# Prompt attention: the probabilities of two key blocks are transposed in a row, and weighted in a row

## The chip, the cores and the metric

The kernel runs on one core of one Trainium2 chip. The metric is the device time of one execution in microseconds (us); lower is better. The engines of a core run side by side, each through its own list of instructions in order, and wait for each other by semaphores: TensorE (PE, matrix products and its weight loads PEld), VectorE (DVE), ScalarE (ACT), GpSimd (POOL) and SyncE (SP), which here only starts DMA transfers.

## The reference

Two layers of an encoder trunk (width 1024). Each layer projects the normalised input once, feeds four branches with it (a recurrent branch, latent attention, spatial gating, pooling), gates them and projects back. There are 1024 prompt tokens and 8 groups of 16 sample tokens, 1152 in all. The change touches the attention of the prompt:

```
def mla_attend(q_nope, q_rope, qpos, k_nope, krope, v, kpos):
    s = (einsum('bqhd,bkhd->bhqk', q_nope, k_nope)
         + einsum('bqhd,bkd->bhqk', q_rope, krope)) / sqrt(96)
    mask = (qpos // 64)[:, None] >= (kpos // 64)[None, :]
    s = where(mask, s, -1e30)
    pr = softmax(s, axis=-1)
    return einsum('bhqk,bkhd->bqhd', pr, v)
```

Four heads, queries in 8 blocks of 128, values 64 wide per head, all in fp32. Block `qt` of queries sees keys up to `(qt + 1) * 128`.

## The kernel before

Tokens lie in columns, in three groups of 384. A layer goes through its input projections (one 128-wide piece of features after the other, `project`, L245), with the branches' own work strung between them, then through the prompt attention, then through the output projection. The prompt attention is the loop at L1394 to L1412.

Its unit is a row: one query block of one head (32 rows, L1260). A row has one or two key blocks of up to 512 keys. `scores(r)` (L1269) multiplies queries by keys on TensorE into PSUM tiles `b` (four of them), finds the maximum on VectorE (`mx`, `ng`), and takes the exponential on ScalarE (L1295) into one of four slots of probabilities (`Pb`, printed as X). A new row is started only when as many slots are free as it has key blocks.

`turn(u, b)` (L1299) takes key block `b` of two rows (two heads, `hh` 0 and 1) and transposes the probabilities on TensorE, 128 by 128 at a time, into PSUM tiles `pj`, of which there are two: one for each head. The head 0 tile is copied to SBUF by VectorE (L1311), the head 1 tile by ScalarE (L1313), into a ring of four tiles `PTb` (L1195).

`weigh(u, b)` (L1316) multiplies the transposed probabilities by the values, into the PSUM tile `st` that holds the outputs of a pair of query blocks. For each 128 keys there are two products (L1325), one per head. Each has 64 output rows: head 0 goes to partitions 0 to 63, head 1 to 64 to 127. `settle` (L1330) divides by the sums and gates the result when a pair of query blocks is done.

The order in the program: for each (u, b), first the scores of as many rows as fit, then `weigh` of the turn before, then `turn`. A scheduler in the framework then places the instructions of each engine; it can set an instruction ahead of others when it finds its inputs ready earlier, so what stands in an engine's list is not the program's order word for word. There are 24 turns per layer, an even number for each pair of query blocks.

Of the kernel before, what the change touches and what calls it, by code (L numbers as in the profile page):

```python
# [48 lines left out]
def tile_trunk(ctx: ExitStack, tc: tile.TileContext, *aps):  # L49
# [25 lines left out]
    def mm(out, lhsT, rhs, start=True, stop=True):  # L75
        return PE.matmul(out, lhsT=lhsT, rhs=rhs, start=start, stop=stop, skip_group_check=True)  # L76
# [39 lines left out]
    def st():  # L116
        return ps_st.tile([128, 512], F32, tag="st", name=nm("st"))
# [7 lines left out]
    def go(lane, gen):  # L125
        lanes.setdefault(lane, deque()).append(gen)
# [15 lines left out]
    def tick():  # L142
        for lane in list(lanes):
            step(lane)

    def finish(*names):
        while any([step(n) for n in names]):
            pass
# [196 lines left out]
    for l in range(L):  # L345
# [919 lines left out]
        def widths(qt):  # L1265
            n = (qt + 1) * 128
            return [min(512, n - 512 * b) for b in range((n + 511) // 512)]

        def scores(r):  # L1269
            pr, s, h = rows[r]  # L1270
            qt = pr[s]
            if h == 0 and s == 0:
                sums[pr] = smp.tile([128, 2, 2, 4], F32, tag="sums", name=nm("sums"), bufs=2)
                Po.memset(sums[pr], 0.0)
            mx = smp.tile([128, 2], F32, tag="mx", name=nm("mx"), bufs=4)
            banks = []
            ws = widths(qt)
            for b, w in enumerate(ws):
                pc = pb()
                mm(pc[:, :w], qcols(h, qt * 128, 128), Kt[h][:, 512 * b:512 * b + w])  # L1280
                if b == len(ws) - 1:
                    V.memset(pc[0:64, w - 64:w], NEG)
                V.tensor_reduce(out=mx[:, b:b + 1], in_=pc[:, :w], axis=AX.X, op=ALU.max)  # L1283
                banks.append((pc, w))
            ng = smp.tile([128, 1], F32, tag="ng", name=nm("ng"), bufs=4)
            if len(ws) == 2:
                V.tensor_scalar(out=ng, in0=mx[:, 0:1], scalar1=mx[:, 1:2], scalar2=-SCALE,  # L1287
                                op0=ALU.max, op1=ALU.mult)
            else:
                V.tensor_scalar(out=ng, in0=mx[:, 0:1], scalar1=-SCALE, scalar2=None, op0=ALU.mult)  # L1290
            prow[r] = []
            for b, (pc, w) in enumerate(banks):
                slot = free.pop(0)
                P = Pb[slot]
                A.activation(out=P[:, :w], in_=pc[:, :w], func=AF.Exp, scale=SCALE, bias=ng,  # L1295
                             accum_out=sums[pr][:, b, s, h:h + 1])
                prow[r].append((slot, w))

        def turn(u, b):  # L1299

            trow[u, b] = []
            for hh in range(2):
                slot, w = prow[2 * u + hh][b]
                ptp = pj()
                for j in range(w // 128):
                    PE.transpose(ptp[:, j * 128:(j + 1) * 128], Pb[slot][:, j * 128:(j + 1) * 128], ident)  # L1306
                free.append(slot)
                PT = PTb[ring["t"] % len(PTb)]
                ring["t"] += 1
                if (hh if w > 128 else u % 2) == 0:  # L1310
                    V.tensor_copy(out=PT[:, :w], in_=ptp[:, :w])  # L1311
                else:
                    A.activation(out=PT[:, :w], in_=ptp[:, :w], func=AF.Copy)  # L1313
                trow[u, b].append(PT)

        def weigh(u, b):  # L1316
            pr, s, h = rows[2 * u]
            if h == 0 and s == 0 and b == 0:
                St["po"] = st()
            o = St["po"][:, s * 256 + h * 64:s * 256 + h * 64 + 128]  # L1320
            pts = trow.pop((u, b))
            n = pr[s] + 1
            for j in range(4 * b, min(4 * b + 4, n)):
                for hh in range(2):
                    mm(o[64 * hh:64 * hh + 64], Vt[j][:, (h + hh) * 64:(h + hh + 1) * 64],  # L1325
                       pts[hh][:, j % 4 * 128:j % 4 * 128 + 128], j == 0, j == n - 1)
            if h == 2 and s == 1 and 4 * b + 4 >= n:
                go("f", settle(pr, St["po"]))

        def settle(pr, po):  # L1330

            sm = sums.pop(pr)
            V.tensor_tensor(out=sm[:, 0], in0=sm[:, 0], in1=sm[:, 1], op=ALU.add)
            V.reciprocal(out=sm[:, 0], in_=sm[:, 0])
            Po.tensor_copy(out=Ob[0].rearrange("p (a f) -> p a f", a=8),
                           in_=sm[:, 0].rearrange("p s h -> p (s h)").unsqueeze(2).broadcast_to([128, 8, 64]))
            yield
            pt = pj()
            for j in range(4):
                PE.transpose(pt[:, j * 128:(j + 1) * 128], Ob[0][:, j * 128:(j + 1) * 128], ident)  # L1340
            A.activation(out=Ob[1], in_=pt, func=AF.Copy)
            V.tensor_tensor(out=Ob[1], in0=po, in1=Ob[1], op=ALU.mult)
            for j in range(4):
                s, i = divmod(j, 2)
                gs = gB[i][:, pr[s] * 128:pr[s] * 128 + 128]
                Po.tensor_tensor(out=gs, in0=gs, in1=Ob[1][:, j * 128:(j + 1) * 128], op=ALU.mult)
# [23 lines left out]
        def operand(g):  # L1370
            if g == 2:
                finish("f")
            h = xp.tile([128, 8, G], F32R, tag="xh", name=nm("yh"))
            lo = xp.tile([128, 8, G], F32R, tag="xl", name=nm("yl"))
            for n, k in enumerate(out_order):
                if k < 2:
                    src = AR[k][g][:, :, 0, :]
                    hv, lv_ = chv(h[:, k, :]), chv(lo[:, k, :])
                else:
                    if k < 4:  # L1380
                        src = gB[k - 2][:, gcols(g)]
                    else:
                        src = s_tile("ea", EA)
                        SY.dma_start(out=src, in_=ysp[:, k - 4, gcols(g)])
                    hv, lv_ = h[:, k, :], lo[:, k, :]
                A.activation(out=hv, in_=src, func=AF.Copy)
                eng = Po if k % 2 else V
                eng.tensor_tensor(out=lv_, in0=src, in1=hv.bitcast(F32), op=ALU.subtract)
                if n == 3:
                    yield  # L1390
            yh.append(h)
            yl.append(lo)

        ahead, before = 0, None  # L1394
        for u in range(16):
            for b in range(len(widths(rows[2 * u][0][rows[2 * u][1]]))):
                while ahead < 32 and len(widths(rows[ahead][0][rows[ahead][1]])) <= len(free):
                    scores(ahead)
                    ahead += 1
                if before:  # L1400
                    weigh(*before)
                turn(u, b)
                before = u, b
                tick()
            if u == 8:
                finish("q")
            if u == 12:
                go("o", operand(0))
                go("o", operand(1))
        weigh(*before)  # L1410
        finish("n")
        go("o", operand(2))  # L1412

# [191 lines left out]
```

## Time and profile before

| | |
|---|---|
| median of 3 runs | 1441.29 us (1440.91 to 1446.11) |
| profiled execution | 1443.43 us |
| its span in the trace | 1441.6 us |
| TensorE busy | 1357.0 us (94%) |
| VectorE, ScalarE, GpSimd busy | 779.5, 747.8, 466.8 us |
| prompt attention, layer 1 | about 551 to 635 us of the span |
| prompt attention, layer 2 | about 1255 to 1338 us of the span |

The trace is of the profiled execution. Its time has 1.83 us around the span (launch and end). A product in fp32 stands in the trace as two matrix instructions, so a run of 8 products of `weigh` is a row with x16; a transposition is one instruction. Short idle times of TensorE show in the distance between starts, since the ends of matrix instructions are modelled.

### The profile page before, as it was taken

The page shows a single profiled execution, that of the slowest core. Times are in us where ns is not written, and L with a number is a line of the kernel's source. Part 1 is how long each engine was busy: PE and PEld are TensorE (multiplying, and loading weights), DVE is VectorE, ACT ScalarE, POOL GpSimd, SP SyncE. Part 2 cuts the span into 40 slices and gives each one's busy share as a digit, 9 for nine tenths or more (in the row PEclk, how much of TensorE's full clock was granted, in tenths as well). Part 3 has the DMA queues.
Part 4 walks back from the last instruction along what each step waited for, and adds up shares of the span by engine and source line. Part 5 has one row for each costly group of instructions (what it writes and reads, how often), then busy time and mean ns, then how long its engine had stood idle before and what let it go on. Part 6 is the DMA issues. An engine that isn't in the chain of part 4 may idle for free.

```text
span 1441.6 us, 26906 instructions
## 1 busy us (share of the span) xinstructions
PE 1357.0 (94%) x9962; PEld 1157.6 (80%) x9962; DVE 779.5 (54%) x1758; ACT 747.8 (52%) x2013; POOL 466.8 (32%) x600
## 2 busy tenths in 40 slices
PE   4799989999999998999989998999999999899999
PEld 3678878888988886679977788788789788766998
DVE  6875954435235567752287858444532375777211
ACT  6762234655466677652257621555653676766210
POOL 4514404426411023232162333332653111422320
PEclk9899999999999999999999999999999999999999
DMA  7212241210211213033300123321122111131222
GB/s 222 53 34 70 67 101 42 65 46 25 92 50 65 66 37 118 15 103 106 93 29 30 47 67 68 89 70 50 32 73 68 53 58 58 47 101 45 76 93 77
DMA packets 116596, 97.40 MB, mean 68 GB/s; under 512 B 46129, under 2 KB 111345, under 8 KB 116465
## 3 DMA queue, kind: packets, MB, share of 16 engines
q1 hardware_dynamic: 76776, 73.74, 17.8%
q10 hardware_dynamic: 39688, 21.94, 5.1%
q8 instruction: 79, 1.29, 0.4%
q14 instruction: 53, 0.43, 0.1%
HBM read 71.48 MB, written 24.16 MB: 66 GB/s over the span
## 4 chain that ended last, share of the span: by engine, by line
PE 67%; DVE 17%; DMA 5%; ACT 4%; issue 3%; POOL 3%; SPq 0%; ACTq 0%; DVEq 0%; POOLq 0%
PE pj L76 40%; PE b L76 14%; PE st L76 8%; DMA nd<-ns 3%; PE pj L1306 3%; DVE ea L278 2%; DVE m L540 2%; DVE m L542 2%; DMA tt<-dd 1%; POOL sp L99 1%; PE b L588 1%; DVE gn L730 1%; DVE ea L170 1%; DMA m<-nds 1%; DVE m L793 1%
## 5 line engine op out<-in xcount | busy, mean ns | idle before, releaser
L76 PE MATMUL pj<-xh,wh 128*128 128x384 f32 x1152 | 415.1, 361 | 19.3 <-ACT xh L280 7.3
L76 PE MATMUL pj<-xl,wh 128*128 128x384 f32 x1152 | 395.6, 343 | 3.8 <-POOL xl L282 2.8
L76 PE MATMUL pj<-xh,wl 128*128 128x384 f32 x1152 | 395.7, 344 | 0.0
L242 POOL TENSOR_TENSOR wl<-wr,wh 128x256 fp32r<-128x256 f32 x200 | 159.4, 805 | 459.6 <-ACT wh L241 398.0
L76 PEld LDWEIGHTS pj<-xh,wh 128*128 128x128 f32 x1152 | 220.9, 192 | 44.4 <-ACT sho L400 13.5
L76 PEld LDWEIGHTS pj<-xl,wh 128*128 128x128 f32 x1152 | 221.1, 192 | 12.1 <-POOL xl L282 4.8
L76 PEld LDWEIGHTS pj<-xh,wl 128*128 128x128 f32 x1152 | 220.6, 192 | 4.3 <-issue 3.1
L76 PE MATMUL pj<-yh,wh 128*128 128x384 f32 x384 | 129.3, 337 | 2.4 <-DVE x L1428 2.4
L76 PE MATMUL pj<-yh,wl 128*128 128x384 f32 x384 | 128.6, 335 | 0.0
L76 PE MATMUL pj<-yl,wh 128*128 128x384 f32 x384 | 128.3, 334 | 0.0
L241 ACT ACTIVATE wh<-wr 128x256 fp32r<-128x256 f32 x200 | 81.3, 414 | 80.7 <-PE pj L76 38.7
L242 POOL TENSOR_TENSOR wl<-m,wh 128x256 fp32r<-128x256 f32 x56 | 43.5, 789 | 102.8 <-ACT wh L241 84.9
L76 PEld LDWEIGHTS pj<-yh,wh 128*128 128x128 f32 x384 | 72.1, 188 | 3.7 <-DVE x L1428 2.7
L76 PEld LDWEIGHTS pj<-yl,wh 128*128 128x128 f32 x384 | 72.1, 188 | 0.1
L76 PEld LDWEIGHTS pj<-yh,wl 128*128 128x128 f32 x384 | 72.1, 188 | 0.1
L1295 ACT ACTIVATE X<-b,ng 128x512 f32<-128x512 f32 (+3 forms) x96 | 55.0, 577 | 25.6 <-DVE ng L1287 21.4
L76 PE MATMUL b<-sp,cr 128*128 128x384 f32 (+3 forms) x192 | 59.5, 385 | 3.2 <-POOL sp L99 2.8
L1283 DVE TENSOR_REDUCE mx<-b 128x1 f32<-128x512 f32 (+3 forms) x96 | 53.0, 555 | 9.7 <-PE b L76 8.0
L76 PEld LDWEIGHTS st<-X,X 128*64 128x64 f32 x576 | 35.1, 136 | 27.4 <-ACT X L1313 7.6
L1424 DVE TENSOR_TENSOR pt<-pj,pt 128x384 f32<-128x384 f32 x24 | 13.4, 557 | 80.6 <-PE pj L76 80.6
L241 ACT ACTIVATE wh<-m 128x256 fp32r<-128x256 f32 x56 | 22.2, 412 | 60.9 <-PE pj L76 59.2
L1306 PE MATMUL pj<-cm,X 128*128 128x128 f32 x288 | 48.0, 286 | 5.2 <-ACT X L1295 5.2
(307 smaller groups left out, 2584.9 us busy)
## 6 DMA issues: line engine op xcount, KB each, us to landing
wr<-in_win_dram SPq DMA_DIRECT2D x176, 128.0 KB
m<-in_wout_dram SPq DMA_DIRECT2D x12, 512.0 KB
x<-in_xT_dram SPq DMA_DIRECT2D x12, 384.0 KB
ysp<-m ACTq DMA_DIRECT2D x24, 192.0 KB
pt<-in_xT_dram SPq DMA_DIRECT2D x24, 192.0 KB
ea<-ysp SPq DMA_DIRECT2D x24, 192.0 KB
x1d<-x ACTq DMA_DIRECT2D x24, 192.0 KB
pt<-x1d SPq DMA_DIRECT2D x24, 192.0 KB
```

What stands on the lines that cost most here:

```text
L76: return PE.matmul(out, lhsT=lhsT, rhs=rhs, start=start, stop=stop, skip_group_check=True)
L99: by[1].tensor_tensor(out=view(lo), in0=src, in1=view(hi.bitcast(F32)), op=ALU.subtract)
L170: V.tensor_tensor(out=acc, in0=acc, in1=q, op=ALU.add)
L241: A.activation(out=h, in_=r, func=AF.Copy)
L242: Po.tensor_tensor(out=lo, in0=r, in1=h.bitcast(F32), op=ALU.subtract)
L278: V.scalar_tensor_tensor(out=t, in0=xs[k // 2][:, k % 2, :], scalar=vcs[:, l, V_NG + k:V_NG + k + 1], in1=rs, op0=ALU.mult, op1=ALU.mult)
L540: V.tensor_tensor(out=tm, in0=full[:, 0:s + 1, s:s + 1].broadcast_to([np_, s + 1, w]), in1=NTt[0:np_, s:s + 1, s + 1:n].broadcast_to([np_, ...
L542: V.tensor_tensor(out=full[:, 0:s + 1, s + 1:n], in0=full[:, 0:s + 1, s + 1:n], in1=tm, op=ALU.add)
L588: PE.transpose(pt[:, i * 128:(i + 1) * 128], KB[i][g][:, cl].rearrange("p a t -> p (a t)"), ident)
L1283: V.tensor_reduce(out=mx[:, b:b + 1], in_=pc[:, :w], axis=AX.X, op=ALU.max)
L1295: A.activation(out=P[:, :w], in_=pc[:, :w], func=AF.Exp, scale=SCALE, bias=ng, accum_out=sums[pr][:, b, s, h:h + 1])
L1306: PE.transpose(ptp[:, j * 128:(j + 1) * 128], Pb[slot][:, j * 128:(j + 1) * 128], ident)
```

## The change

`weigh` is no longer called for one turn ahead of each next turn, but for the two turns before, ahead of every second turn. So the lists of `weigh` come in pairs, and so do the turns.

```
-        ahead, before = 0, None
+        ahead, before, turns = 0, [], 0
         for u in range(16):
             for b in range(len(widths(rows[2 * u][0][rows[2 * u][1]]))):
                 while ahead < 32 and len(widths(rows[ahead][0][rows[ahead][1]])) <= len(free):
                     scores(ahead)
                     ahead += 1
-                if before:
-                    weigh(*before)
+                if turns % 2 == 0:
+                    while before:
+                        weigh(*before.pop(0))
                 turn(u, b)
-                before = u, b
+                turns += 1
+                before.append((u, b))
                 tick()
...
-        weigh(*before)
+        while before:
+            weigh(*before.pop(0))
         finish("n")
         go("o", operand(2))
```

No instruction is added or taken away; the ring of four `PTb` tiles holds two turns. Counted in TensorE's list, the 144 products of `weigh` of one layer stand in 35 runs before, of 2, 2, 1, 7, 4, 1, 7, 1, 3, 1, 3, 4, 1, 7, 1, 1, 1, 7, 2, 6, 6, 8, 8, 8, 6, 1, 7, 6, 1, 7, 8, 1, 7, 1 and 7 products, and in 14 afterwards, of 1, 3, 12, 1, 11, 8, 10, 10, 12, 16, 14, 14, 16 and 16. Both layers have the same lists.

TensorE in the middle of layer 1 before, units 7 and 8 (`pj<-cm,X` are transpositions, `b<-m,X` scores, `st<-X,X` products of `weigh`):

```order
L1306 MATMUL pj_6736<-cm,X_6132 128x128 x4
L76 MATMUL st_6638<-X_6133,X_6132 64x128
L1306 MATMUL pj_6768<-cm,X_6133 128x128
L76 MATMUL b_6775<-m_4641,X_6131 128x384
L76 MATMUL st_6638<-X_6133,X_6132 64x128 x7
L1306 MATMUL pj_6771<-cm,X_6133 128x128
L76 MATMUL b_6783<-m_4642,X_6131 128x384
L76 MATMUL st_6638<-X_6133,X_6132 64x128 x2
```

The same place now:

```order
L1306 MATMUL pj_6736<-cm,X_6132 128x128 x4
L76 MATMUL b_6753<-m_4640,X_6131 128x384
L1306 MATMUL pj_6760<-cm,X_6133 128x128
L1306 MATMUL pj_6763<-cm,X_6133 128x128
L76 MATMUL b_6767<-m_4641,X_6131 128x384
L76 MATMUL b_6775<-m_4642,X_6131 128x384
L76 MATMUL st_6669<-X_6133,X_6132 64x128 x10
```

The three runs of 1, 7 and 2 products, with transpositions and scores between them, have become one run of 10 behind both turns.

TensorE at the end of layer 1's attention, the last unit (the first `pj<-yh,wh` is the output projection):

```order
 L1306 MATMUL pj_7188<-cm,X_6132 128x128 x4
 L1306 MATMUL pj_7194<-cm,X_6132 128x128 x4
-L76 MATMUL st_6964<-X_6133,X_6132 64x128
-L1306 MATMUL pj_7208<-cm,X_6133 128x128 x4
-L76 MATMUL st_6964<-X_6133,X_6132 64x128 x7
-L1306 MATMUL pj_7214<-cm,X_6133 128x128 x4
-L76 MATMUL st_6964<-X_6133,X_6132 64x128
+L1306 MATMUL pj_7200<-cm,X_6133 128x128 x4
+L1306 MATMUL pj_7206<-cm,X_6133 128x128 x4
+L76 MATMUL st_6997<-X_6133,X_6132 64x128 x16
```

The last two turns now follow each other with nothing between them, and both lists of `weigh` follow as one run of 16; before, the last 7 products stood behind the first three of the output projection.

SyncE's list moves too, since buffers come free in another order. Before, in layer 1, the block of output weights m_7513 stood behind twelve loads `ea<-ysp` of the gated branch outputs, of which the last two stand here:

```order
L1384 DMA ea_7280<-ysp_316 128x384
L1384 DMA ea_7284<-ysp_316 128x384
L201 DMA m_7513<-in_wout_dram 128x1024
L201 DMA m_7627<-in_wout_dram 128x1024
L201 DMA m_7741<-in_wout_dram 128x1024
```

Now it stands ahead of the first of the twelve:

```order
L201 DMA m_7513<-in_wout_dram 128x1024
L1384 DMA ea_7026<-ysp_316 128x384
L1384 DMA ea_7030<-ysp_316 128x384
L1384 DMA ea_7034<-ysp_316 128x384
L1384 DMA ea_7038<-ysp_316 128x384
```

So one transfer of 512 KB is issued ahead of the loads that ScalarE's copies `yh<-ea` (L1386) wait for.

## Rows read from the trace of the kernel before

**Rows 1.** The page: the span, and busy time of each engine.
```profile
span 1441.6 us, 26906 instructions
PE 1357.0 (94%) x9962; PEld 1157.6 (80%) x9962; DVE 779.5 (54%) x1758; ACT 747.8 (52%) x2013; POOL 466.8 (32%) x600
```

**Rows 2.** Busy times by stretch: layer 1's attention in three parts, then output projection.
```profile
core 0: us, PE busy (x) PEld busy (x) DVE busy (x) ACT busy (x) POOL busy (x), PEclk, DMA share, GB/s
551.00:572.00 21.00, 19.37 (x124) 12.75 (x125) 16.63 (x58) 14.57 (x49) 5.48 (x8) 1.00 0.36 114
572.00:596.00 24.00, 24.00 (x155) 14.72 (x156) 15.18 (x49) 13.86 (x43) 4.20 (x8) 1.00 0.19 56
596.00:633.00 37.00, 35.88 (x264) 22.45 (x262) 26.18 (x58) 22.67 (x58) 10.88 (x17) 1.00 0.20 58
645.00:720.00 75.00, 75.00 (x435) 75.00 (x434) 19.15 (x35) 18.62 (x42) 17.74 (x24) 1.00 0.38 107
```

**Rows 3.** TensorE's waits, 546 to 645 us: total us, times, longest.
```profile
PE pj L1306 <- ACT X L1295: 2.7, 4, 1.2
PE b L76 <- POOL sp L99: 1.1, 2, 0.9
PE b L76 <- ACT pt L213: 0.8, 2, 0.6
```

**Rows 4.** The same of layer 2, 1265 to 1365 us.
```profile
PE pj L1306 <- ACT X L1295: 1.3, 3, 0.5
```

**Rows 5.** The chain that ended last: start us, us from the piece before's end.
```profile
573.54 0.58 PE st L76 x6
...
592.86 0.81 PE st L76 x12
...
599.96 1.02 PE st L76 x16
...
621.05 1.72 PE b L76 x4
622.77 0.44 PE pj L1306 x4
623.21 0.36 PE st L76 x2
623.57 0.59 PE pj L1306 x4
624.16 1.02 PE st L76 x14
625.18 0.59 PE pj L1306 x4
```

**Rows 6.** Timeline: transpositions of one turn, and the copies behind them.
```profile
604.47 0.66 PE L1306 MATMUL pj<-cm,X 128*128 128x128 f32 x4
605.17 0.69 DVE L1311 COPY X<-pj 128x512 f32<-128x512 f32 x1 [0.61 <-PE pj L1306]
605.83 0.60 PE L1306 MATMUL pj<-cm,X 128*128 128x128 f32 x4
606.46 0.60 ACT L1313 ACTIVATE X<-pj 128x512 f32<-128x512 f32 x1 [0.47 <-PE pj L1306]
```

**Rows 7.** Timeline: from the last scores to the transposition that waits for them.
```profile
627.78 0.69 DVE L1283 TENSOR_REDUCE mx<-b 128x1 f32<-128x512 f32 x1
628.75 0.69 ACT L1295 ACTIVATE X<-b,ng 128x512 f32<-128x512 f32 x1 [2.36 <-DVE ng L1287]
629.59 0.66 PE L1306 MATMUL pj<-cm,X 128*128 128x128 f32 x4 [0.49 <-ACT X L1295]
```

**Rows 8.** Timeline: the loads of gated outputs on SyncE's queue, and their first use.
```profile
564.07 3.66 SPq L1384 DMA_DIRECT2D ea<-ysp  x8
570.49 0.95 ACT L1386 ACTIVATE yh<-ea 128x384 fp32r<-128x384 f32 x2
```

**Rows 9.** DMA rate, 540 to 640 us in 40 slices of 2.5 us.
```profile
GB/s 0 3 210 88 125 0 13 72 79 52 269 321 148 165 241 125 0 0 0 0 0 3 7 0 3 0 0 0 3 7 210 0 210 113 97 118 98 0 0 0
```

## The prediction, made before the changed kernel was run

> **What bounds the kernel now.** I read the page first, then the busy times by stretch, then TensorE's waits, then the chain of work that ended last, and the timeline only at single places. On the page TensorE is busy 94% of the span and no other engine above 54% [rows 1]. By stretch the same holds for the place of the change: in layer 1's attention TensorE is busy 79.25 of 82 us (19.37, 24.00 and 35.88), VectorE 57.99 and ScalarE 51.10, and the granted clock is full (1.00, the 2.4 GHz level) [rows 2]. The output projection behind it has TensorE busy 75.00 of 75.00 us [rows 2]. So what TensorE saves in the attention should reach the end, unless it waits instead. Its waits there are few: 2.7 us in four pieces for an exponential in layer 1, of which 1.2 us are the stage's first, and 1.3 us in layer 2 [rows 3, 4]; 1.9 us more of layer 1 are at the end of the query work that runs into the stage [rows 3].
>
> The bound is thus TensorE's own time, and the question is what the order of its instructions costs. The chain shows it. A run of `weigh` with x2 takes 0.36 us, x6 0.58, x12 0.81, x16 1.02, and x14 also 1.02 [rows 5]. The x2 is one product, of one head; x16 are eight products, four for each head. So time goes by pairs (two heads side by side), about 0.22 us a pair, (1.02 - 0.36) / 3, and a run that begins or ends with a lone product pays a whole pair for it: 1 product costs as much as 2, and 7 as much as 8. What is left of each run is 0.36 - 0.22 = 0.14, say 0.15 us of entry. There is an exit as well: four transpositions behind scores take 0.44 us, and the same four behind a run of `weigh` 0.59 [rows 5], 0.15 us more. Each run of `weigh` therefore costs about 0.30 us beside its pairs, wherever it stands.
>
> **The change part by part.** No instruction comes or goes; each keeps its shape.
>
> Runs: 35 become 14 in each layer. 21 x 0.30 = 6.3 us a layer. None of it lies beside other work, since TensorE is the bound.
>
> Lone products: rounding each run up to pairs gives 83 pairs before (22 runs of odd length) and 74 now (4 of odd length). 9 x 0.22 = 2.0 us a layer. Together 8.3 us a layer, 16.5 us in two layers.
>
> The size of a long run is the first unknown, as no row has more than x16, and the change makes x20 to x32. Bounds: if a long run pays its 0.30 us again with every eight products, the 14 runs count as 24 and the gain is 11 x 0.30 + 2.0 = 5.3 us a layer, 10.6 in all; from below, nothing beyond the pairs can be saved, so 16.5. I take 16.5, because from x6 to x16 the pairs alone set the rows.
>
> Waits that go: the three short waits for an exponential in layer 1 (2.7 - 1.2 = 1.5 us) and those of layer 2 (1.3 us). The clearest is ahead of a turn that had the scores of its row only one `weigh` and one half turn earlier: reduction of 0.69 us at 627.78, exponential at 628.75, transposition at 629.59 after 0.49 us of waiting [rows 7]. With two lists of `weigh` in front such a place has up to 8 pairs, 8 x 0.22 + 0.15 = 1.9 us, as cover where it had 1.02. So some of these 2.8 us should go. But others come.
>
> Waits that are added: the second turn of two has only scores between it and the first. It writes the two `pj` tiles that the first has just filled. The copy ends 0.73 us after the transpositions' end on VectorE (605.17 + 0.69 against 604.47 + 0.66) and 0.63 us on ScalarE (606.46 + 0.60 against 605.83 + 0.60) [rows 6]. The second turn writes the head 0 tile first, when the head 1 transpositions (0.44 us) have passed: with nothing between, 0.73 - 0.44 = 0.3 us of wait. With the scores of a row between (0.86 us for 512 keys, half of the 1.72 [rows 5]) it is covered. In TensorE's new list scores (in one place query products too) stand between the two turns of each pair but the last, so 0.3 us a layer. What waits behind the head 0 transposition there is only the rest of the turn. The products behind both turns find the first turn's copies long done, and the second's are covered by the first's products.
>
> ScalarE and VectorE take their copies and exponentials in a new order. An exponential that stands behind one such piece of 0.6 or 0.69 us comes that much later, and what it can cost is what its cover lacks. I allow two such delays a layer, 1.5 us beside the 0.3, and bound them by 0 and 4. Against that stand the 1.5 and 1.3 us that may go; I count half of them. Net: 2 x 1.8 - 1.4 = +2.2 us.
>
> SyncE: the 512 KB of m_7513 are now issued ahead of the loads `ea<-ysp`. Those were issued from 564.07, and their first use on ScalarE is at 570.49, 6.4 us later [rows 8]. At the 269 and 321 GB/s of those slices [rows 9], 512 KB take 1.6 to 2.0 us. ScalarE would stop at that copy, with exponentials and copies behind it, only if the loads landed less than 2 us ahead of their use. Between 0 and 2 us a layer; I take 0, as eight loads were on the way together and the first of them is the one used first.
>
> Sum: the profiled execution took 1443.43 us, 1441.6 of it span. 1443.43 - 16.5 + 2.2 = 1429.1 us. That execution lies 2.1 us above the median of the runs, 1441.29, so on the scale of the medians 1427.
>
> **The rivals.**
>
> Copies out of PSUM become the bound (slower). Two turns in a row use both `pj` tiles twice, and the copies stand in line behind exponentials. The Trainium skill, page TensorEngine Tiling (Array Packing), section PSUM Bottleneck, says that packing speeds up TensorE but not the emptying of PSUM, so that the copies may become the bottleneck. In mean load the rows are against it: VectorE's 57.99 us and ScalarE's 51.10 us [rows 2] would fill 78% and 69% of a stage shortened to 74 us. As a delay it is possible: a copy on ScalarE behind one exponential of 512 keys costs 0.69 us more [rows 7], so 0.3 + 0.69 = 1.0 us for a second turn, and behind two 1.7. There are 12 second turns a layer, 24 in all. The change loses from 16.5 / 24 = 0.69 us for each. At 1.0 us: 1441.3 - 16.5 + 24 = 1449. Against it: scores of 0.86 us or more lie between the turns in all places but two. Chance 0.05.
>
> The entry and exit are not the run's (no change). If the 0.30 us appear again inside long runs in other form, as waits for copies or for weight loads, only the 2 x 2.0 us of lone products remain: 1441.3 - 4 = 1437. For it speaks that no long run is in the trace; against it that the same 0.15 us show behind runs of x2, x14 and x16 alike [rows 5]. Chance 0.09.
>
> ScalarE stops at the loads behind m_7513: 2 x 2 us lost, and 1430. Chance 0.10.
>
> The change does not do what it says: the scheduler still sets single products ahead. In the two first pairs of turns it does (runs of 1, 3, 12, 1 and 11), and this is in the count; elsewhere its list is what will run, so there is no more of it.
>
> **How the numbers follow.** 0.76 for the forecast, whose own range is 1422 (every wait gone: 16.5 + 2.8) to 1433 (4 us of new waits a layer). With the rivals at 1430 (0.10), 1437 (0.09) and 1449 (0.05), a range that leaves out at most 2 in 10 is 1420 to 1436. A change of 0.5% (7.2 us, about what a measurement of this kernel can tell from none) ends at 1434.1. Faster holds nearly all of the forecast and the loads' case: 0.86; within 0.5%: 0.10; slower: 0.04.
>
> **What would show it.** Right: the chain's rows of `weigh` come as x20 to x32, with 1.9 us for x32 (8 x 0.22 + 0.15); about 14 such runs a layer; the stage is some 7 to 8 us shorter in each layer and the output projection behind it still has no idle time. Waits for an exponential stay below 3 us a layer. Wrong: new waits of transpositions for the copies at L1311 or L1313, a wait of ScalarE's copies `yh<-ea` for a DMA, or x32 taking 2.2 us and more.

## The result, and the profile after

| | before | after |
|---|---|---|
| median of the runs | 1441.16 us (1440.91 to 1446.11) | 1431.41 us (1427.92 to 1431.9) |
| ratio | | 0.9904, interval 0.9884 to 0.9923 |
| profiled execution | 1443.43 us | 1431.8 us |

The kernel is about 1% faster. The ratio and its interval are the comparison's own; the quotient of the two medians, of four runs each, is 0.9932. On a kernel of 1443 us the ratio means 13.9 us, where the difference of the two medians is 9.8. A second measurement of the same kernel in a later session (e7 below) gave 1427.45 us and 0.9898 (0.9883 to 0.9913). The forecast was 1427, its range 1420 to 1436.

The page of the changed kernel: span, and busy time of each engine. TensorE keeps its 94% [rows 1].

```profile
span 1430.0 us, 26928 instructions
PE 1344.6 (94%) x9962; PEld 1158.8 (81%) x9962; DVE 779.1 (54%) x1758; ACT 748.6 (52%) x2013; POOL 464.6 (32%) x600
```

Busy times by stretch, layer 1's attention in three parts and then the output projection (columns as in [rows 2]):

```profile
549.87:570.00 20.13, 20.01 (x138) 13.90 (x139) 17.13 (x56) 15.69 (x51) 6.08 (x8) 1.00 0.43 138
570.00:594.00 24.00, 23.89 (x174) 15.82 (x173) 19.49 (x59) 17.53 (x50) 7.91 (x14) 1.00 0.13 40
594.00:623.10 29.10, 27.68 (x244) 19.05 (x242) 19.56 (x45) 17.75 (x45) 6.13 (x11) 1.00 0.23 74
623.10:698.00 74.90, 74.90 (x435) 74.87 (x434) 21.38 (x36) 21.90 (x49) 22.63 (x30) 1.00 0.36 104
```

The attention is over after 73.2 us, and the output projection behind it still has no idle time. Its last part as a chain (start us, us from the piece before's end), which answers to [rows 5]:

```profile
603.08 1.68 PE st L76 x28
604.76 0.59 PE pj L1306 x4
605.35 0.86 PE b L76 x2
606.21 0.44 PE pj L1306 x4
...
616.89 1.90 PE st L76 x32
618.79 0.60 PE pj L1306 x4
619.39 0.02 issue
619.42 0.70 DVE X L1311
620.12 0.04 issue
620.16 1.09 PE pj L1306 x8
621.26 1.90 PE st L76 x32
```

x28 takes 1.68 and x32 1.90 us: 7 and 8 pairs of 0.22 us and one entry of 0.15, as forecast. Four transpositions take 0.59 us behind weigh and 0.44 behind scores: the exit is there, but less often. And at 619.42 stands the one new wait that was worked out beforehand, a second turn with nothing but the first in front of it, for the copy of L1311. All of TensorE's waits from 545 to 623 us (total us, times, longest), which answer to [rows 3, 4]; layer 2, from 1248 to 1326 us, has the same three and the fourth below:

```profile
PE pj L1306 <- ACT X L1295: 2.3, 2, 1.2
PE b L76 <- POOL sp L99: 0.9, 1, 0.9
PE pj L1306 <- DVE X L1311: 0.3, 1, 0.3
PE st L76 <- DVE X L1311: 0.3, 1, 0.3
```

1.2 us of the exponential's 2.3 are again the stage's first, and the 0.9 for `sp` stands ahead of the first transposition. The other 1.1 us are one new wait, at 598.25, where the maximum that its exponential needs stands on VectorE behind an unrelated subtraction (L1388):

```profile
594.79 0.97 DVE L1388 TENSOR_TENSOR yl<-ar,yh 128x384 fp32r<-128x384 f32 x1
595.69 0.68 DVE L1283 TENSOR_REDUCE mx<-b 128x1 f32<-128x512 f32 x1
596.37 0.11 DVE L1282 MEMSET b<- 64x64 f32 x1
596.52 0.56 DVE L1283 TENSOR_REDUCE mx<-b 128x1 f32<-128x384 f32 x1
597.11 0.21 DVE L1287 TENSOR_SCALAR ng<-mx 128x1 f32<-128x1 f32 x1
```

### The profile page after: what moved, and what is told of

Its sections match the earlier page's. It is cut to its first block, busy times and chain, and to the rows that moved or that the text cites. A ratio compares the mean times of both kernels' runs of the same rounds, so it can differ in the third digit from the quotient of the medians.

```text
span 1430.0 us, 26928 instructions
## 1 busy us (share of the span) xinstructions
PE 1344.6 (94%) x9962; PEld 1158.8 (81%) x9962; DVE 779.1 (54%) x1758; ACT 748.6 (52%) x2013; POOL 464.6 (32%) x600
## 3 DMA queue, kind: packets, MB, share of 16 engines
q1 hardware_dynamic: 76776, 73.74, 17.7%
## 4 chain that ended last, share of the span: by engine, by line
PE 65%; DVE 19%; ACT 4%; issue 4%; DMA 4%; POOL 2%; ACTq 1%; SPq 0%; DVEq 0%; POOLq 0%
PE pj L76 40%; PE b L76 14%; PE st L76 7%; DVE ea L278 2%; DVE m L542 2%; DVE m L540 2%; PE pj L1306 2%; DMA nd<-ns 2%; PE b L588 1%; DVE ea L170 1%; DVE kb L484 1%; DVE mx L1283 1%; DVE xl L282 1%; DVE m L793 1%; DVE m L387 1%
## 5 line engine op out<-in xcount | busy, mean ns | idle before, releaser
L1306 PEld LDWEIGHTS pj<-cm,X 128*128 128x128 f32 x288 | 32.7, 141 | 23.1 <-ACT X L1295 10.9
L282 POOL TENSOR_TENSOR xl<-ea,xh 128x384 fp32r<-128x384 f32 x30 | 38.3, 1295 | 40.2 <-ACT xh L280 40.1
```

Of the source, the lines that this page charges most:

```text
L282: eng.tensor_tensor(out=lo[:, k, :], in0=t, in1=h[:, k, :].bitcast(F32), op=ALU.subtract)
```

## Where the time went, stretch by stretch

I cut each span at the first transposition of each attention (L1306) and 0.24 us behind its last product of weigh. In brackets, for the start and the stretch between, us at half of TensorE's clock (1.2 GHz), from the granted clock:

| | start | attention 1 | between | attention 2 | end |
|---|---|---|---|---|---|
| before | 551.8 (20.5) | 83.0 | 620.5 (13.7) | 82.8 | 103.5 |
| after | 549.9 (17.1) | 73.3 | 629.5 (27.3) | 73.5 | 104.0 |
| changed kernel again (e7) | 546.6 (13.7) | 73.3 | 626.4 (27.3) | 73.5 | 104.0 |
| layer 1 only (e1) | 548.4 (20.5) | 73.2 | 627.1 (27.3) | 82.8 | 103.5 |
| layer 2 only (e2) | 548.3 (17.1) | 83.1 | 621.3 (13.7) | 73.2 | 104.0 |

The program up to the first attention is the same in all of them; its 546 to 552 us are the spread between executions. Each attention loses 9.7 and 9.3 us. Of that 0.5 us is only moved, since three products of the output projection stood inside it before and stand behind it now (between and end, 0.5 us more each). So 9.2 and 8.8 us are saved, 18.0 in all. But of layer 1's part 5.4 to 8.5 us come back before layer 2's attention begins (626.4 to 629.5 - 0.5 - 620.5). Layer 2's part reaches the end whole. These are single profiles; on the scale of whole times e1 below gains 5.9 us of the 9.3 that its attention saves, so 3.4 come back.

Where they come back is seen by cutting the stretch once more, at a wait that all kernels have, of a product behind the copies into `sho` (L400). The two parts, of before, after, e1 and e2 (columns as in [rows 2]):

```profile
634.90:846.59 211.69, 199.90 (x1147) 180.35 (x1147) 119.12 (x209) 98.02 (x232) 75.54 (x91) 0.98 0.22 65
846.59:1255.40 408.81, 393.03 (x3277) 344.20 (x3278) 214.18 (x509) 224.81 (x629) 136.04 (x171) 1.00 0.22 62
```

```profile
623.10:838.25 215.15, 201.79 (x1152) 182.46 (x1150) 119.82 (x209) 98.24 (x232) 74.96 (x91) 0.97 0.22 64
838.25:1252.60 414.35, 397.82 (x3282) 348.59 (x3283) 214.69 (x509) 225.18 (x630) 135.85 (x171) 0.98 0.21 61
```

```profile
621.70:835.39 213.69, 200.72 (x1151) 181.64 (x1151) 119.74 (x209) 97.95 (x232) 75.76 (x91) 0.97 0.22 64
835.39:1248.80 413.41, 398.35 (x3277) 349.31 (x3278) 214.39 (x509) 224.78 (x629) 135.80 (x171) 0.98 0.22 61
```

```profile
631.40:843.20 211.80, 199.93 (x1148) 180.35 (x1147) 119.19 (x209) 97.99 (x232) 75.42 (x91) 0.98 0.23 65
843.20:1252.60 409.40, 393.73 (x3281) 344.74 (x3281) 214.64 (x509) 224.81 (x630) 135.53 (x171) 1.00 0.22 62
```

In the second part TensorE runs the same instructions, but is busy 4.8 and 5.3 us longer where layer 1's attention is changed (397.82 and 398.35 against 393.03), at a mean granted clock of 0.98 instead of 1.00; the part is 5.5 and 4.6 us longer. With e2 it is as before. These us are TensorE's clock, not a wait. In the first part the two kernels lose 3.5 and 2.0 us, of which 0.5 is the moved work.

At the cut itself the wait is longer, by 1.4 us. The rows of before, then of after: SyncE issues a piece of weights, ScalarE waits for it, and a product waits for ScalarE's copies behind it:

```profile
841.91 0.33 SPq L238 DMA_DIRECT2D wr<-in_win_dram  x1
844.49 0.42 ACT L241 ACTIVATE wh<-wr 128x256 fp32r<-128x256 f32 x1 [1.24 <-DMA wr<-in_win_dram]
846.59 0.44 PE L76 MATMUL pj<-xh,wh 128*128 128x384 f32 x1 [1.98 <-ACT sho L400]
```

```profile
832.22 0.33 SPq L238 DMA_DIRECT2D wr<-in_win_dram  x1
836.15 0.42 ACT L241 ACTIVATE wh<-wr 128x256 fp32r<-128x256 f32 x1 [2.63 <-DMA wr<-in_win_dram]
838.25 0.69 PE L76 MATMUL pj<-xh,wh 128*128 128x384 f32 x1 [3.37 <-ACT sho L400]
```

The load is used 2.6 us behind its issue before, 3.9 after; TensorE's wait goes from 2.0 to 3.4 us, and behind the long wait the clock is at half. The stretches around the end of that wait, before and after (granted clock in the third column from the end):

```profile
843.00:849.00 6.00, 4.02 (x24) 3.70 (x23) 2.48 (x7) 1.91 (x7) 3.94 (x5) 1.00 0.56 102
849.00:852.50 3.50, 3.50 (x22) 3.50 (x21) 1.03 (x7) 1.06 (x3) 0.08 (x1) 1.00 0.71 159
```

```profile
832.00:838.20 6.20, 2.89 (x17) 2.56 (x15) 3.51 (x7) 1.54 (x6) 2.65 (x6) 1.00 0.43 86
838.20:841.60 3.40, 3.35 (x10) 3.35 (x11) 0.62 (x1) 0.53 (x3) 2.06 (x3) 0.50 0.78 128
```

TensorE, idle for 3.3 of 6.2 us, does 10 products in the next 3.4 us, at 1.2 GHz; before, idle for 2.0 of 6.0 us, it did 22 in 3.5. In the profiles of the experiments it goes like this: where the wait was 1.9 to 2.4 us (before, e2, e3, e5) no half clock stood behind it; where it was 3.4 to 3.7 (after, e1, e4, e6, e7, e9 to e12), one did each time, and in e8, with two waits of 2.2 and 2.5 us, as well. The length of the wait alone does not decide it: one of 2.4 us some 120 us earlier had no half clock behind it in before (729.7) and had one in after (718.5).

The longer wait also explains only a part of the loss. The other stretches at half clock of the second part stand behind waits that are as long as in the kernel before (3.0 us for L542, 1.8 for L857), but for one behind 1.6 us for `tt<-dd` in after. In e6 and e11, which have the new order of the turns and the long wait too, most of them are missing: 6.3 and 6.6 us at half clock against 13.5 in after and 16.1 in e1, and the second part is only 1.4 and 2.1 us longer than before. In e6 the whole stretch between takes 623.5 us, so 2.5 us come back and not 5 to 8.

## The experiments

**Each layer alone (e1, e2).** The new order in one layer only:

```
-                if turns % 2 == 0:
+                if turns % 2 == 0 or l == 1:      # e1 (e2: l == 0)
```

> The change in layer 1 alone; layer 2 as before. Theory A (each attention saves its own 9 us, and the time lost again between the attentions is stretches at half TensorE clock that fall on other places of layer 2's input projections once layer 1 ends earlier): layer 1's attention 73.2 us long instead of 82.3, layer 2's 82; the stretch between them longer than before's 621 us only where the granted clock of a stretch is lower; total 1441.2 - 9.1 + 0 to 8, so 1432 to 1440. Rival B (the changed order of buffers and transfers itself makes the work behind layer 1's attention slower, at full clock): the stretch between is 629 us as in the changed kernel and the total 1440, without more low clock.

> The change in layer 2 alone; layer 1 as before. Theory A: layer 2's attention 73.4 us instead of 82.1; nothing behind it but the output projection, in which TensorE never waits, so the whole 8.7 us reach the end: 1432.5, within 2 us for stretches at low clock ahead of it. Rival B (work behind a changed attention gets slower): the output projection of layer 2 takes longer than before's 103.5 us and the total is 1437 or more.

Measured: 1437.49 us, ratio 0.9959 (0.9946 to 0.9972) for layer 1; 1434.31 us, 0.9941 (0.9924 to 0.9959) for layer 2; before, in the same session, 1443.25. By the ratios 5.9 and 8.5 us, together 14.4, where the whole change has 13.9 on that scale (0.0096 x 1443). The saving inside the attention is the same in both (9.8 and 9.6 us by the table); only layer 1's has a stretch behind it in which to lose it again.

**More work at the seam (e3, e4).** The seam is the end of layer 1's output projection and the start of layer 2's input projections. My clock theory was that the moment at which layer 2's work arrives decides where half clock falls. The changed kernel with 24 or 48 more products in layer 1's output projection, each written over by the next product:

```
+                    if n == 0 and keys[0][0] == 0 and keys[0][1] >= NF:
+                        for _ in range(1):                    # e4: 2
+                            mm(ps[:, :G], wh, hi[g][:, k, :], True, False)
```

> The changed kernel, with 24 more matrix products of 0.173 us (the first of each accumulation issued twice) in layer 1's output projection: 4.2 us of TensorE time more, after which layer 2 begins 4.2 us later. Theory A: what is lost between the attentions depends on when layer 2's projections arrive, so the total is not the changed kernel's 1431.4 + 4.2 = 1435.6 but differs from it by the clock, between 1429 and 1437. Rival B: 1435.6 within 1 us.

> The same with 48 more products, 8.3 us: layer 2 begins nearly when it does in the kernel before. Theory A: layer 2's projections meet the clock as in the kernel before, so 6 to 8 us come back and the total is 1432 to 1434, hardly above the changed kernel in spite of 8.3 us more work. Rival B: 1431.4 + 8.3 = 1439.7.

Measured: 1433.21 us, 0.9927 (0.9914 to 0.9940), and 1436.37 us, 0.9953 (0.9940 to 0.9967). By the ratios, against 0.9904, the products cost 3.3 and 7.1 us of the 4.2 and 8.3 us that they take: little or nothing came back. The stretch between the attentions without them, 634.0 - 4.2 = 629.8 and 637.9 - 8.3 = 629.6 us, is as long as the changed kernel's 629.5 (626.4 in e7). So moving layer 2's front back by about what the attention had saved does not bring back the old stretch. That speaks against the form of my clock theory by which only the moment decides; e4 has the long wait for `sho` too (3.64 us).

**The price of a run (e5, e6).** One word in weigh, in the kernel before (e5) and the changed one (e6):

```
-                for hh in range(2):
+                for hh in (1, 0):
```

> The kernel before with one word changed: weigh issues head 1's product ahead of head 0's for each 128 keys. In TensorE's list the runs of weigh go from 35 to 24 a layer, none of odd length, and the pairs from 83 to 72; the order of the turns stays as before. Theory of the run's price (0.30 us of entry and exit a run, 0.22 us a pair): 11 x 0.30 + 11 x 0.22 = 5.7 us a layer, so each attention 83 - 5.7 = 77.3 us; 11.4 us in all, of which up to 6 may be given back between the attentions: ratio 0.992 to 0.996. Rival, entry and exit alone: 3.3 us a layer, attention 79.7. Rival, pairs alone: 2.4 us a layer, attention 80.6. Rival, the gain of the change came from its new order of the turns: nothing, attention 83, ratio 1.000.

> The changed kernel with the same one word changed. Runs 14 to 13 a layer, odd ones 4 to 0, pairs 74 to 72. Theory of the run's price: 0.3 + 2 x 0.22 = 0.7 us a layer, attention 73.3 to 72.6, 1.5 us in all: ratio 0.989 to 0.990 against the kernel before. Rival, a long list of weigh has no further entries or half pairs to lose: nothing, attention 73.3, ratio as the changed kernel's.

Measured: e5 1435.99 us, 0.9954 (0.9938 to 0.9969); attentions 78.7 and 78.5 us. e6 1427.38 us, 0.9892 (0.9876 to 0.9907); attentions 72.9 and 72.9 us. So e5 saves 4.3 us a layer where the run's price said 5.7, and is beyond both rivals that take one half of the price alone. I summed, from start to start, what stands between the first product of each run and the next other instruction: 24.8 us before, 19.4 in e5, 18.4 after, 17.9 in e6. By 0.15 us a run and 0.22 a pair it should be 23.5, 19.4, 18.4 and 17.8: all as worked out, but for 1.3 us in before. Most of these are stops: a transposition behind a run (0.63 us of recorded wait at 615.06) and scores behind a run (0.20 at 567.70) wait for ScalarE, and a run of six products from 619.19 on takes 1.21 us instead of 0.81. Part of what e5 lacks are waits, 3.9 us in layer 1's attention where before has 3.1 (total us, times, longest):

```profile
PE pj L1306 <- ACT X L1295: 3.1, 4, 1.2
PE st L76 <- ACT X L1313: 0.6, 2, 0.3
PE b L76 <- POOL sp L99: 0.2, 1, 0.2
```

Now weigh follows its turn with one key block of scores between (x2, from 609.43), and waits for ScalarE's copy at 610.77. Behind two turns in a row no wait for L1313 is recorded (after, e6, e7). And e6 gains 0.4 to 0.6 us in each attention, where 0.7 was worked out, too little to show in the whole time.

**The changed kernel again (e7).** No edit.

> The changed kernel once more, unchanged. Its ratio again 0.988 to 0.992. It shows by a second profile whether the 629.5 us between the two attentions (620.5 in the kernel before) come again. If they are the order's doing, 629 again. If they come from the stretches at half clock, they move with them: 616 us and half of what stands at half clock (27 us in the first profile).

Measured: 1427.45 us, 0.9898 (0.9883 to 0.9913). The stretch between the attentions took 626.4 us with 27.3 us at half clock: neither of the two expectations. The half clock comes again, the length is 3.1 us less; 1.6 us of that is a wait for a transfer (`tt<-dd`) that only the first profile has.

**Keeping TensorE busy at the seam (e8, e9, e10).** The changed kernel waits 2.4 and 3.5 us at the seam, with half clock behind it. e8 puts products that nobody reads there:

```
+    def fill(n, w, x):
+        t = pb()
+        for _ in range(n):
+            mm(t[:, :G], w, x)
...
+                if keys[0] == (0, NF + 6) and g == 2 and fi == f0:
+                    fill(14, pieces[4 * fi][0][:, 0, :], hi[g][:, 0, :])
+                if keys[0] == (1, WDAD) and g == 0 and fi == f0 + 1:   # e8: fi == f0, constants
+                    fill(18, pieces[4 * fi][0][:, 0, :], hi[g][:, 0, :])
```

e9 and e10 also issue the sums of squares of layer 2's second and third group later; e10 has `fill(0, ...)`:

```
+        for _ in range((0, 0, 2, 3)[g + 1] if l else 0):
+            yield
...
-        mm(ss[:, :G], ones, acc)
+        behind(tail[0] if l else None, lambda: mm(ss[:, :G], ones, acc))
```

> The changed kernel, with products that nobody reads where TensorE waits at the seam of the two layers: 14 of 384 columns ahead of the last group's last output pieces (wait of 2.4 us), 18 ahead of layer 2's first input piece (wait of 3.5 us); at 0.174 us each 2.4 and 3.1 us, so inside the waits. Clock theory: behind these waits the changed kernel ran at half clock for 3.4 and 6.8 us (718.7 to 722.1 and 735.8 to 742.6), and with TensorE busy it stays at the 2.4 GHz level: 3.5 to 5 us less between the attentions (629.5 to 625), ratio 0.986 to 0.988. Rival, the time between the attentions is the order's own: nothing gained, 0 to 1 us lost, ratio 0.990 to 0.992.

> The changed kernel, with 32 products that nobody reads at the two places of the seam where TensorE waits (2.4 us ahead of the last group's last output pieces, 14 products; 3.5 us ahead of layer 2's second input piece, 18 products; 0.174 us each, so 2.4 and 3.1 us, inside the waits), and with the next sums of squares (st<-ea) issued two and three ticks later, so that they do not stop TensorE behind the products. Clock theory: TensorE is busy across the waits, and the stretches at half clock behind them (718.7 to 722.1 and 735.8 to 742.6 in the changed kernel) come at the 2.4 GHz level: 10 us less at half clock, 3.5 to 5 us less between the attentions than in the same kernel without the products (e10). Rival, the time between the attentions is the order's own: no difference to e10, or up to 1 us more.

> The same kernel as e9 without its 32 products: the changed kernel with the two sums of squares issued later. Both theories: the ratio of the changed kernel, 0.988 to 0.992, with waits of 2.4 and 3.5 us at the two places. By the clock theory stretches at half clock stand behind them in most executions.

Measured: e8 1428.95 us, 0.9902 (0.9887 to 0.9917). It left the question open: the scheduler set the sum of squares (`st<-ea`) ahead, and TensorE now waited for that, 2.43 and 3.44 us, behind the added products. e9 1424.42 us, 0.9852 (0.9827 to 0.9876); e10 1422.38 us, 0.9844 (0.9821 to 0.9867). The seam in e9, then in e10:

```profile
711.00:718.00 7.00, 6.98 (x40) 6.66 (x40) 6.99 (x11) 3.62 (x8) 4.37 (x4) 1.00 0.15 56
...
725.00:732.00 7.00, 7.00 (x42) 7.00 (x41) 7.00 (x8) 2.78 (x6) 5.89 (x6) 1.00 0.00 0
732.00:739.00 7.00, 7.00 (x38) 5.94 (x37) 4.55 (x9) 5.65 (x14) 2.02 (x2) 1.00 0.08 28
```

```profile
713.30:717.30 4.00, 1.57 (x10) 1.25 (x9) 4.00 (x8) 1.57 (x3) 2.05 (x2) 1.00 0.05 18
717.30:720.70 3.40, 3.40 (x12) 3.40 (x11) 3.32 (x5) 2.19 (x5) 2.60 (x3) 0.50 0.26 94
...
730.00:734.30 4.30, 1.72 (x11) 1.43 (x10) 4.30 (x6) 1.24 (x3) 3.25 (x4) 1.00 0.00 0
734.30:737.70 3.40, 3.40 (x12) 3.40 (x11) 2.69 (x5) 2.88 (x7) 1.34 (x2) 0.50 0.18 63
```

With the products TensorE is busy and the clock stays at 1.00; without them it waits 2.4 and 2.6 us and then runs 3.4 us at 0.50, twice. In these two profiles, then, the clock behind this place stayed full where TensorE had been busy and fell where it had waited. But the full clock brought only 1.2 us up to the wait for `sho` (208.66 us from the attention's end against 209.85), where 3.5 to 5 were expected, and nothing in the whole time. The rows give the likely reason: VectorE is busy all of the 7.00, 4.00 and 4.30 us, and both of e10's waits end with its work (`x`, L1444). At the seam it is the bound, and a slow TensorE behind it costs little. From the wait for `sho` to layer 2's attention e9's TensorE was busy 1.7 us less than in e10's (397.23 and 398.89), but stood idle 4.9 us longer, of which 2.4 us for `tt<-dd`.

What gained was e10's delay alone, 5 and 9 us by the medians of the changed kernel's two sessions and this one, 8 to 9 by the ratios. There the sum of squares of the third group stopped TensorE once more (0.9 us, behind a wait of 3.5); with it later, the waits at the seam are 2.4 and 2.6 us.

**Side by side or not (e11).** All products of head 0, then all of head 1, in each list:

```
-            for j in range(4 * b, min(4 * b + 4, n)):
-                for hh in range(2):
+            for hh in range(2):
+                for j in range(4 * b, min(4 * b + 4, n)):
```

> The changed kernel, but in each run of weigh all products of head 0 come first and then all of head 1, so that the two heads' products (output rows 0 to 63 and 64 to 127) no longer alternate. Theory of the pairs (0.22 us for two products because the two heads lie side by side): each product pays 0.22 us alone, 144 instead of 74 a layer, 70 x 0.22 = 15.4 us more; x32 takes 16 x 0.22 + 0.15 = 3.7 us instead of 1.9, each attention 73.3 to 88.7 us, the whole near 1458. Rival, 0.11 us is the price of a product wherever it stands: x32 stays at 1.9 us, attention 73 us, 1428.

Measured once: 1435.65 us, attentions 77.2 and 77.1 us. Its chain has

```profile
619.14 2.50 PE st L76 x32
```

between the two theories' 3.7 and 1.9 us. So the halves do work side by side, and a product alone is dearer than half a pair. But they need not alternate one by one: in the trace head 1's first product starts 0.5 us behind head 0's first, when head 0's third is in work, and then the two lists run together. The changed kernel shows the overlap directly: in its x32 the instructions start two by two, 0.006 us apart, and a new two every 0.11 us. The price of a pair is right where heads alternate, and too high a price for a lone product in the middle of a list.

**Both edits (e12).** The changed kernel with e6's word and e10's delay:

```
+        for _ in range(g + 1 if l and g else 0):
+            yield
...
-                for hh in range(2):
+                for hh in (1, 0):
```

> The changed kernel with the two small edits that gained or cost nothing so far put together: head 1's product ahead of head 0's in weigh (e6), and layer 2's second and third sums of squares issued two and three ticks later (e10 without its unused tile). If the two gains add: each attention 72.9 us (73.3 in the changed kernel), between the attentions 623 us (626 to 629 in the changed kernel), ratio 0.983 to 0.985. If e10's gain was a matter of where the stretches at half clock fell in its executions, ratio 0.989 as in e6.

Measured: 1420.11 us (1416.99 to 1423.95), ratio 0.9842 (0.9820 to 0.9863); attention 1 took 72.9 us, the stretch between 623.4, attention 2 73.5. It beats both kernels: by the ratio 22.8 us below before, where the changed kernel has 13.8 to 14.7. From e10 it can't be told apart, so that the two gains add is not shown: layer 2's attention has a wait of 0.53 us for an exponential that e6 does not have.

## Why the prediction was right, and where it was not

- **The bound, and what runs and pairs cost: right.** 0.15 us of entry and 0.22 us a pair give the runs' own time in four kernels within 0.1 us, once those 1.3 us are taken out. The other 0.15 us, which the prediction puts behind the run, lie on both sides of it by the starts in the trace: a transposition or score ahead of a run takes 0.09 us longer (0.20 against 0.11), and the first transposition behind it 0.06 (0.165 against 0.109). The sum is the same. The rival by which the 0.30 us come again inside long runs is refuted by x32 in 1.90 us. For the entry and the exit the Trainium skill has the likely reason, page TensorEngine Tiling (Array Packing), section Tiling Modes: a change of the tiling mode drains the engine. It names no price; here it is 0.30 us for going in and out. No run here shows that the drain is the reason.
- **The waits: wrong by 2.6 us.** I took 2.2 us more for both layers. Between the first transposition, its own wait left out, and the last product of weigh TensorE waits 1.4 us in layer 1 where it waited 1.9 (0.35 of the 1.9 us that the prediction puts ahead of the stage lie in it), and 1.7 in layer 2 where it waited 1.6. That is 0.4 us less in all. The 0.3 us at L1311 was right to the place and the size (0.35 by the timeline). Of the two delayed exponentials a layer there is one, of 1.07 us.
- **What is saved in the attention should reach the end: the step that failed.** It saved 18.0 us where the sum had 16.5 - 2.2 = 14.3: runs and pairs give 16.5, the waits 0.4, and 0.8 are the stops inside a run of six products, 0.4 us in each layer, together 17.7. Of layer 1's share 5.4 to 8.5 us came back between the attentions in the two profiles, and by the ratio about 4 of the 18.0. I had looked for idle time of TensorE only as far as the output projection; the waits of layer 2's front, which are not TensorE's work, stand 90 us behind it. That 1427 came within 0.5 and 4.4 us of the two measured medians is thus in part luck: two errors of opposite sign.
- **The rivals.** Copies as the bound: the copies made TensorE wait 0.3 us in layer 1 and 0.6 in layer 2, not 12. Loads behind m_7513: ScalarE never waited for one (issued from 561.45, first use at 566.24). It does what it says: 14 runs a layer.
- **The late load.** The load at the wait for `sho` is used some 1.3 us later in the kernels with layer 1's turns in the new order (all of them but e3, where it is 0.4). The trace's DMA packets show where most of it lies. Of the load's 128 packets of 1 KB, the last eight begin in after only at 2.66 us behind the issue, and end at 3.05; in before all 128 are done at 2.17. Ahead of these eight, at 2.10 us, stands a packet of 8 KB of instructions (queue q14 of the page). It comes 2.1 to 2.4 us behind the issue in the ten kernels with the late load, whose last packet ends at 3.0 to 3.3 us, at 1.5 in e3 (2.4), and at 4.0 to 4.1, when the load is done, in before, e2 and e5 (2.1 to 2.2). No run varied this alone, so the packet is the likely cause and not a shown one.
- **Still open.** Why that packet and the load meet in the new order; the kernels that move only weigh's products or layer 2 (e5, e2) do not have it, and e4 speaks against the moment alone. And why the same wait of 1.80 us for L857 had half clock behind it in seven profiles (after, e1, e3, e7, e8, e10, e12) and none in the other seven, before, e2 and e6 among them: what else the engine did around it was not varied.

## What to carry to other kernels

Products of 64 output rows among products of 128 are worth collecting: count the runs in TensorE's list and multiply by the entry and exit that the chain shows. Where the two heads alternate, let a run begin and end with a whole pair; which head comes first can decide that. A saving in a busy stage has to be followed to the next stage that waits: there it can meet a later load or a lower clock. What half clock costs depends on which engine is the bound: at the seam, with VectorE busy throughout, 6.8 us of it cost about 1.2 us (e9, e10), and behind the wait for `sho` 10 and 13 us more of it kept TensorE busy 4.8 and 5.3 us longer (after, e1).

## What the runs showed of the hardware

- Two products for different output halves need not be neighbours in the list to run together: x32 in blocks of four per head took 2.50 us (e11), against 1.90 in the changed kernel, where they alternate and start 0.006 us apart. The Trainium skill, page TensorEngine Tiling (Array Packing), section Tiling Modes, says that tiles execute independently; the trace agrees.
- The same 128 KB load at the same place of the program took 2.5 to 2.6 us from issue to use in before, e2 and e5, 3.0 in e3, and 3.9 to 4.3 in the other kernels. In e3 and these others an 8 KB packet of instructions was moved while the load was under way; in before, e2 and e5 it came behind the load's end.
- Products that nobody reads kept the granted clock at 1.00 across two waits (e9), without a gain in time over the same kernel without them (e10).
